# Attention values of two heads: one 128-column product, or two 64-column products on halves of the array

## The chip, the cores and the metric

The kernel runs on one core of one Trainium2 chip. The metric is the device time of one execution in microseconds (us); three runs of the kernel before gave 1727.19, 1726.89 and 1725.22 us, median 1726.89.

## The reference, cut to what matters

A two-layer encoder trunk on 512 tokens of width 1024. Each layer has three branches (a gated linear recurrence A, a spatial gating B, a windowed attention C), a gated merge, and an MLP. The change lies in branch C: eight query heads of 64 columns share two key/value heads of 64 columns; each block of 128 queries sees its own block of keys and the neighbours.

```python
def window_attention(q, k, v, sink):
    ...
    scores = jnp.einsum('bnqhgd,bnkhd->bnhgqk', qb, kb).astype(jnp.float32) * (C_HDIM ** -0.5)
    ...
    p = jnp.exp(scores - m)
    p = p / (jnp.sum(p, axis=-1, keepdims=True) + jnp.exp(sink_l - m))
    o = jnp.einsum('bnhgqk,bnkhd->bnqhgd', p.astype(v.dtype), vb)
    return o.reshape(bsz, s_len, C_QW)
```

Query head j uses the first value head and query head 4+j the second; the kernel handles the two as pair j.

## The kernel before, in words

Activations lie feature by token: 128 partitions of features, 512 tokens along the free axis. Large products are done as three float32r products of high and low parts (`mm3`, L200 to L202; the same pattern at L242 to L244 and L406 to L408). Weights come from DRAM in 512 KB pieces (L175), are rounded by ScalarE (ACT, L195) and the remainder is taken by VectorE (DVE, L196).

Branch C runs with pieces of branch A (`a_head`, L534 to L633) and the gates of branch B (`merge_b`, projections at L200 to L202 into `gz` and `yB`) in one stage per layer. For each pair j (four) and each query block n (four):

- `c_scores`: two float32r products into a bank (L912, L913) for each head, mask and maximum on DVE (L915), exponentials and sums on ACT (L919, L921), the division on DVE (L926) for one head and on ACT (L928) for the other.
- `c_out`: for each of the two heads, TensorE (PE) transposes the nb blocks of probabilities into a bank (L941), and ACT copies them into `pT`, a tile [128 keys, block, head, 128 queries] (L942). nb is 2 for the first and last query block and 3 for the two others. Then the value products (L946) and the copies into `yc` (L948).

In `c_out`, `cv[:, kb:kb + P]` holds 128 keys by 128 value columns: 64 columns of the first value head, 64 of the second. The product of L946 takes all 128 columns as weights and streams both heads' probabilities, 256 columns, so its output is 128 partitions by 256 columns. Only two quarters of it are wanted: the first head's queries on partitions 0 to 63, the second head's on 64 to 127. L948 copies these two quarters, 64 partitions by 128 columns each, into the two halves of `yc[j]`.

These products are float32; the trace shows each as two records of MATMUL with a weight load (LDWEIGHTS, listed as PEld) each. There are 4 x 4 query blocks per layer with 40 products, 80 products in both layers.

PSUM has eight banks in four groups of two; transposes of `pT` and the product `po` share group "s". `pT` has one buffer. A list scheduler sets each engine's order over the whole program, by priorities (`later`, `hp`) and its own simulated timeline; so an edit at one place can move other instructions of the stage.

Of the kernel before, what the change touches and what calls it, by code (L numbers as in the profile page):

```python
# [12 lines left out]
P = 128  # L13
# [46 lines left out]
def trunk(tc, xT, xt, ws, vec, fnb, bsb, snk, wst, rope, cmask, amask, ident, out):  # L60
    nc = tc.nc
# [30 lines left out]
    def nm(s):  # L92
        ctr[0] += 1
        return f"{s}_{ctr[0]}"

    def T(tag, name, dt=F32):
        where = part[HOME[tag]] if tag in HOME else sb
        return where.tile([P, S], dt, tag=tag, bufs=SLOTS[tag], name=nm(name))
# [17 lines left out]
    def PT(tag, name):  # L116
        return ps.tile([P, S], F32, tag="p_" + tag, bufs=BANKS[tag], name=nm(name))
# [557 lines left out]
    for l in range(DEPTH):  # L675
# [196 lines left out]
        lo64, hi64 = slice(0, 64), slice(64, 128)  # L872
# [15 lines left out]
        cv = T("ch", "cvt")  # L888
# [10 lines left out]
        yc = []  # L899
# [31 lines left out]
        def c_out(j, n, lo_, nb, Ps):  # L931
            if n == 0:
                yc.append(T("l", "yc"))


            pT = part["br"].tile([P, 3, 2, P], F32, tag="pT", bufs=1, name=nm("pT"))
            for h in range(2):
                pt = PT("s", "pT")
                for b in range(nb):
                    c = slice(b * P, (b + 1) * P)  # L940
                    nc.tensor.transpose(pt[:, c], Ps[h][:, c], id_t)  # L941
                nc.scalar.copy(pT[:, :nb, h], pt[:, :nb * P].rearrange("p (a b) -> p a b", a=nb))  # L942
            po = PT("s", "po")
            for b in range(nb):
                kb = (lo_ + b) * P
                nc.tensor.matmul(po[:, 0:2 * P], cv[:, kb:kb + P], pT[:, b].rearrange("p a b -> p (a b)"), start=b == 0, stop=b == nb - 1)  # L946
            for h, r in enumerate((lo64, hi64)):
                nc.scalar.copy(yc[j][r, n * P:(n + 1) * P], po[r, h * P:(h + 1) * P])  # L948

        def gates(tag, i, fl):  # L950

# [12 lines left out]
        def c_run(j):  # L964
            nonlocal prev
            with later(15000):
                qs = c_q(j)
                for n in range(4):
                    cur = c_scores(j, n, qs)
                    if prev is not None:  # L970
                        c_out(*prev)
                    prev = cur
# [13 lines left out]
        with later(15000):  # L986
            c_out(*prev)
# [281 lines left out]
```

## Time and profile before

| what | value |
|---|---|
| median of the runs | 1726.89 us (1725.22 to 1727.19) |
| span of the profiled execution | 1723.3 us (first to last instruction) |
| median of the runs less that span | 3.6 us |
| instructions | 21981 |
| product of L946 | 160 records, median 379 ns |
| copy of L948 | 64 records, median 260 ns |
| first and last start of L946 | 253.8 and 1293.2 us |

The profile gives no time of its own for the profiled execution beside the span, so the table sets the median of the runs beside it. In the profile each instruction has a line of the kernel, an engine, a start and a duration. PE records are pipelined: a record is longer than the distance from its start to the next one's start. A group of n like records shown as one is as long as n - 1 such distances and one record; the distance is called the pace below. A wait is put down to the instruction that ended it.

### The profile page before, as it was taken

To read this page: it belongs to the slowest core of one execution; us is meant where nothing else is said; L and a number is where in the kernel's file an instruction comes from. 1 tells how busy PE (TensorE), PEld (TensorE's weight loads), DVE (VectorE), ACT (ScalarE), POOL (GpSimd) and SP (SyncE) were. 2 spreads that over 40 slices of the span, in tenths; PEclk is the share of its full clock that TensorE was granted. 3 is DMA by queue.
4 is the path that set the end of the run, shared out by engine and by line. 5 is a ranking of instruction groups with operands and counts; after the bars stand their busy time and mean duration, and the time that the engine had idled before them with its cause. 6 is when DMAs were issued, how large, how long until landed. Compare 5 with 4: busy or idle time off the path is not lost.

```text
span 1723.3 us, 21981 instructions
## 1 busy us (share of the span) xinstructions
PE 1684.3 (98%) x8024; PEld 1405.6 (82%) x8024; DVE 1297.3 (75%) x2024; ACT 1010.9 (59%) x1705; POOL 155.1 (9%) x215
## 2 busy tenths in 40 slices
PE   7999999999999999999999999999989999999997
PEld 5888888888878888888888887888878788888886
DVE  7996987677565768687889869777875667676867
ACT  6665587676335555545666664868882355545464
POOL 1021210100310000000000112001004100000001
PEclk9999999999999999999999999999999999999999
DMA  8243222222555323222334232322216453232311
GB/s 318 75 147 115 84 86 86 86 86 74 185 213 188 98 99 110 98 98 98 135 112 137 95 115 74 104 86 98 86 43 228 169 183 105 98 110 86 122 62 49
DMA packets 58283, 200.04 MB, mean 116 GB/s; under 512 B 7904, under 2 KB 8288, under 8 KB 58176
## 3 DMA queue, kind: packets, MB, share of 16 engines
q1 hardware_dynamic: 44640, 154.72, 26.4%
q0 software_dynamic: 13248, 43.40, 6.9%
q8 instruction: 63, 1.03, 0.3%
q10 hardware_dynamic: 288, 0.52, 0.1%
q14 instruction: 44, 0.36, 0.1%
HBM read 177.64 MB, written 20.97 MB: 115 GB/s over the span
## 4 chain that ended last, share of the span: by engine, by line
PE 82%; DVE 8%; ACT 4%; issue 4%; DMA 1%; POOL 1%; SPq 0%; POOLq 0%; DVEq 0%; ACTq 0%
PE up L201 7%; PE up L200 7%; PE up L202 7%; PE dA L406 3%; PE dA L408 3%; PE dA L407 3%; PE at L534 2%; PE gz L200 2%; PE gz L201 2%; PE gz L202 2%; PE wo L243 2%; PE dC L407 2%; PE dC L406 2%; PE dC L408 2%; PE wo L244 2%
## 5 line engine op out<-in xcount | busy, mean ns | idle before, releaser
L195 ACT CAST wh<-wq 128x1024 fp32r<-128x1024 f32 x196 | 206.2, 1052 | 212.0 <-PE dA L407 49.2
L196 DVE TENSOR_TENSOR wl<-wr,wh 128x1024 fp32r<-128x1024 f32 x171 | 209.4, 1225 | 157.6 <-ACT wh L195 156.9
L195 ACT CAST wh<-wr 128x1024 fp32r<-128x1024 f32 x171 | 179.4, 1049 | 229.5 <-PE up L201 88.4
L196 DVE TENSOR_TENSOR wl<-wq,wh 128x1024 fp32r<-128x1024 f32 x196 | 239.2, 1222 | 87.7 <-ACT wh L195 86.6
L201 PE MATMUL up<-xl,wh 128*128 128x512 f32 x512 | 199.2, 390 | 0.0
L202 PE MATMUL up<-xh,wl 128*128 128x512 f32 x512 | 199.2, 390 | 0.0
L200 PE MATMUL up<-xh,wh 128*128 128x512 f32 x512 | 198.8, 389 | 0.0
L202 PEld LDWEIGHTS up<-xh,wl 128*128 128x128 f32 x512 | 96.1, 188 | 20.0
L200 PEld LDWEIGHTS up<-xh,wh 128*128 128x128 f32 x512 | 96.1, 188 | 20.0
L201 PEld LDWEIGHTS up<-xl,wh 128*128 128x128 f32 x512 | 96.1, 188 | 19.8
L406 PE MATMUL dA<-wh,sh 128*128 128x512 f32 x256 | 99.8, 390 | 0.0
L407 PE MATMUL dA<-wh,sh 128*128 128x512 f32 x256 | 99.7, 389 | 0.0
L408 PE MATMUL dA<-wl,sh 128*128 128x512 f32 x256 | 92.6, 390 | 0.0
L576 DVE TENSOR_TENSOR ex<-ex 128x512 f32<-128x512 f32 x112 | 78.4, 718 | 10.7 <-ACT kt L551 10.0
L548 ACT ACTIVATE qt<-ex 128x512 f32<-128x512 f32 x56 | 37.8, 675 | 53.6 <-DVE ex L576 41.0
L262 POOL TENSOR_TENSOR rs<-ms,mhalf_t 128x4 f32<-128x4 f32 (+2 forms) x15 | 18.9, 1257 | 516.7 <-DVE ms L260 516.7
L534 PEld LDWEIGHTS at<-qt,kt 128*128 128x128 f32 x448 | 57.5, 191 | 8.3 <-ACT kt L551 3.7
L534 PE MATMUL at<-qt,kt 128*128 128x128 f32 x448 | 59.7, 276 | 2.7 <-DVE qt L549 2.0
L406 PEld LDWEIGHTS dA<-wh,sh 128*128 128x128 f32 x256 | 48.0, 188 | 10.0
L408 PEld LDWEIGHTS dA<-wl,sh 128*128 128x128 f32 x256 | 48.1, 188 | 9.9
L407 PEld LDWEIGHTS dA<-wh,sh 128*128 128x128 f32 x256 | 48.1, 188 | 9.9
L200 PE MATMUL gz<-xh,wh 128*128 128x512 f32 x128 | 51.1, 400 | 0.0
(403 smaller groups left out, 4398.2 us busy)
## 6 DMA issues: line engine op xcount, KB each, us to landing
wr<-in_ws_dram SPq DMA_DIRECT2D x171, 512.0 KB, 3.3
wq<-in_ws_dram SPq DMA_DIRECT2D x112, 512.0 KB, 4.2
thd<-zt POOLq DMA_DIRECT2D x32, 256.0 KB, 2.6
th<-thd POOLq DMA_DIRECT2D x32, 256.0 KB, 4.2
mgd<-mg POOLq DMA_DIRECT2D x16, 256.0 KB, 2.4
mcd<-th POOLq DMA_DIRECT2D x16, 256.0 KB, 2.6
mC<-mcd POOLq DMA_DIRECT2D x16, 256.0 KB, 7.2
mB<-mgd POOLq DMA_DIRECT2D x16, 256.0 KB, 5.8
```

What stands on the lines that cost most here:

```text
L195: nc.scalar.copy(hi, raw)
L196: nc.vector.tensor_tensor(lo, raw, hi.bitcast(F32), ALU.subtract)
L200: nc.tensor.matmul(pt, whi, xhi, start=first, stop=False)
L201: nc.tensor.matmul(pt, whi, xlo, start=False, stop=False)
L202: nc.tensor.matmul(pt, wlo, xhi, start=False, stop=last)
L243: nc.tensor.matmul(pts[t], xl, hi[:, c], start=False, stop=False)
L406: nc.tensor.matmul(pt, xh[:, t], hi[:, c], start=start and k == 0, stop=False, skip_group_check=True)
L407: nc.tensor.matmul(pt, xl[:, t], hi[:, c], start=False, stop=False, skip_group_check=True)
L408: nc.tensor.matmul(pt, xh[:, t], lo[:, c], start=False, stop=k == 3, skip_group_check=True)
L534: nc.tensor.matmul(pt[:, c], kk(st), qq[:, c], start=True, stop=True)
L548: nc.scalar.activation(qt.rearrange(shp, b=nb, h=2), e_q, AF.Exp)
L576: nc.vector.tensor_tensor(o_ap, o_ap, ap_of(ex, i_, [[istep, 2]] + z), ALU.add)
```

## The change

Each product of 128 weight columns and 256 streamed columns becomes two products of 64 weight columns and 128 streamed columns. Head 0 goes to partitions 0 to 63 of the bank, head 1 to partitions 64 to 127, both in the same 128 columns. One copy of 128 partitions by 128 columns replaces the two copies.

```diff
             for b in range(nb):
                 kb = (lo_ + b) * P
-                nc.tensor.matmul(po[:, 0:2 * P], cv[:, kb:kb + P], pT[:, b].rearrange("p a b -> p (a b)"), start=b == 0, stop=b == nb - 1)
-            for h, r in enumerate((lo64, hi64)):
-                nc.scalar.copy(yc[j][r, n * P:(n + 1) * P], po[r, h * P:(h + 1) * P])
+                for h, r in enumerate((lo64, hi64)):
+                    nc.tensor.matmul(po[r, 0:P], cv[:, kb + h * 64:kb + h * 64 + 64], pT[:, b, h], start=b == 0, stop=b == nb - 1, skip_group_check=True)
+            nc.scalar.copy(yc[j][:, n * P:(n + 1) * P], po[:, 0:P])
```

In the built program every instruction of PE names the part of the array that it uses: before, all 7520 use 128 rows by 128 columns. After, 7440 do, and the 160 value products use 128 rows by 64 columns, at column 0 or at column 64.

The scheduler moves other rows too. PE, layer 0, pair 0, second query block, before: `po` is the value product, `at` an attention product of branch A, `gz` a gate projection, `pT` a transpose, `sc` scores.

```order
L912 MATMUL sc_2389<-k_399_1920,q_512_2376 128x256
L913 MATMUL sc_2389<-kl_1922,q_512_2376 128x256
L201 MATMUL gz_2968<-xl_156,wh_2964 128x512
L202 MATMUL gz_2968<-xh_155,wl_2965 128x512
L946 MATMUL po_2041<-pT_2030,cvt_1936 128x256
L534 MATMUL at_2222<-qt_2217,kt_2220 128x128 x4
L946 MATMUL po_2041<-pT_2030,cvt_1936 128x256 x2
L941 MATMUL pT_2070<-id_t,sc_2014 128x128 x3
```

The same query block after the change, where its first product stands:

```order
L941 MATMUL pT_2037<-id_t,sc_1982 128x128 x3
L947 MATMUL po_2042<-pT_2031,cvt_1936 64x128
L912 MATMUL sc_2389<-k_398_1919,q_511_2380 128x256
L534 MATMUL at_2214<-q_2196,dg_2212 128x128 x4
L913 MATMUL sc_2389<-kl_1921,q_511_2380 128x256
L201 MATMUL yB_2969<-yl_1705,wh_2915 128x512
```

And further on, where its other five stand:

```order
L534 MATMUL at_2227<-qt_2222,kt_2225 128x128 x4
L912 MATMUL sc_2394<-k_399_1920,q_512_2381 128x256
L913 MATMUL sc_2394<-kl_1922,q_512_2381 128x256
L200 MATMUL gz_2991<-xh_151,wh_2987 128x512
L947 MATMUL po_2042<-pT_2031,cvt_1936 64x128 x5
L941 MATMUL pT_2073<-id_t,sc_2015 128x128 x3
```

Before, the first product needs both heads' transposed probabilities. After, the first product of head 0 needs only head 0's, so it stands apart, and the other five follow later. Over both layers the 160 value products stand in 59 unbroken runs: 26 of one product, 2 of two, 12 of three, 6 of four, 8 of five and 5 of six.

ACT, from the copy of the first query block's result, before (`lb` are small tiles of the recurrence's bounds, `wh` a weight's high part):

```order
L948 COPY yc_1993<-po_2003 64x128 x2
L491 ACT_TABLE_LOAD
L491 ACTIVATE lb_1580<-lb_1580 128x8
L195 CAST wh_2998<-wr_2996 128x1024
L491 ACTIVATE lb_1587<-lb_1587 128x8
L844 ACT_TABLE_LOAD
L844 ACTIVATE gz_2943<-gz_2943 128x512
L554 COPY at_2193<-at_2199 128x512
L548 ACTIVATE qt_2217<-ex_2151 128x512
L551 ACTIVATE kt_2220<-ex_2151 128x512
L942 COPY pT_2030<-pT_2036 128x3x128
```

After:

```order
L948 COPY yc_1993<-po_2003 128x128
L491 ACT_TABLE_LOAD
L491 ACTIVATE lb_1580<-lb_1580 128x8
L554 COPY at_2198<-at_2204 128x512
L548 ACT_TABLE_LOAD
L548 ACTIVATE qt_2222<-ex_2156 128x512
L491 ACT_TABLE_LOAD
L491 ACTIVATE lb_1587<-lb_1587 128x8
L551 ACT_TABLE_LOAD
L551 ACTIVATE kt_2225<-ex_2156 128x512
L195 CAST wh_3021<-wr_3019 128x1024
```

The two copies of the result are one row of 128 partitions, and the functions of branch A now come between the two rows of L491, with table loads on either side. In the whole program ACT has 27 table loads before and 29 after.

## The prediction

> **What bounds the kernel now.** I read the page's busy times first, then the windows of the two stages that hold branch C, then the waits of TensorE (PE) in them, and last the records of the changed lines in order of time.
>
> ```profile
> span 1723.3 us, 21981 instructions
> PE 1684.3 (98%) x8024; PEld 1405.6 (82%) x8024; DVE 1297.3 (75%) x2024; ACT 1010.9 (59%) x1705; POOL 155.1 (9%) x215
> PE 82%; DVE 8%; ACT 4%; issue 4%; DMA 1%; POOL 1%; SPq 0%; POOLq 0%; DVEq 0%; ACTq 0%
> ```
>
> The third row is the chain that ended last. PE is busy 98% of the span and holds 82% of that chain: it is the bound, unless a stage says otherwise. The windows are layer 0's stage, most of layer 1's, and layer 1's end; the columns are length, PE, PEld, DVE, ACT and POOL.
>
> ```profile
> 200.00:460.00 260.00, 257.23 (x1390) 220.51 (x1389) 199.29 (x415) 175.42 (x388) 30.53 (x39) 1.00 0.27 92
> 1090.00:1260.00 170.00, 170.00 (x925) 146.79 (x924) 123.88 (x259) 131.36 (x277) 13.10 (x18) 1.00 0.26 87
> 1260.00:1300.00 40.00, 33.78 (x201) 28.45 (x200) 32.38 (x78) 32.46 (x84) 4.88 (x5) 1.00 0.12 37
> ```
>
> PE is idle for 2.8 us of the first window, never in the second, and 6.2 us in the third, all at the full granted clock (1.00). So whatever the change adds to PE's stream or takes from it reaches the end nearly one for one, except in the last 40 us, where ACT and DVE are each busy for 32 us and PE waits for them:
>
> ```profile
> PE po L946 <- ACT pT L942: 1.7, 1, 1.7
> PE pT L941 <- ACT yc L948: 1.5, 2, 1.1
> ```
>
> The second of these waits is for the copies that the change makes one.
>
> **The change part by part.** *The wide products go.* Their rows, and four pieces of PE's and PEld's order:
>
> ```profile
> L946 PEld LDWEIGHTS po<-pT,cvt x160: 186/190/193, 253.8 to 1293.2; 128*128 128x128 f32 x160
> L946 PE MATMUL po<-pT,cvt x160: 377/379/484, 253.9 to 1293.5; 128*128 128x256 f32 x160
> ...
> L534 PE MATMUL at<-qt,kt x448: 270/275/377, 184.2 to 1290.2; 128*128 128x128 f32 x150
> ...
> 1278.45 0.40 PE L244 MATMUL yC<-wl,yh 128*128 128x512 f32 x1
> ...
> 1278.68 1.05 PE L534 MATMUL at<-qt,kt 128*128 128x128 f32 x8
> ...
> 1279.46 1.17 PEld L946 LDWEIGHTS po<-pT,cvt 128*128 128x128 f32 x6
> 1279.57 1.46 PE L946 MATMUL po<-pT,cvt 128*128 128x256 f32 x6
> ...
> 1285.51 0.97 PEld L534 LDWEIGHTS at<-qt,kt 128*128 128x128 f32 x8 [1.09 <-ACT kt L551]
> 1285.55 1.13 PE L534 MATMUL at<-qt,kt 128*128 128x128 f32 x8 [0.88 <-DVE qt L549]
> ```
>
> The six records at 1279.57 last 1.46 us and one lasts 0.379, so the pace is (1.46 - 0.38) / 5 = 0.216 us. All 160 records hold PE for 160 x 0.216 = 34.6 us; that goes.
>
> *Narrow products come.* 160 products, 320 records by the same two for each, of 128 streamed columns. The nearest row with 128 float32 columns is the product `at`: the eight at 1278.68 give (1.05 - 0.275) / 7 = 0.111 us. If the records pass PE one behind another, 320 x 0.111 = 35.5 us come: 0.9 us more than went, since twice as many stream half as wide. If the two heads' products, which use different column halves and different partitions of the bank, pass beside each other, a slot of 0.111 us is saved wherever a product follows one of the other head. The 160 products stand in 59 unbroken runs, heads alternating, two slots to a product. Within a run the second slot of each is shared with the first of the next, so it takes one slot more than it has products: (160 + 59) x 0.111 = 24.3 us. The trace shows no two records beside each other, so the ends are 35.5 and 24.3. I take 24.3, because nothing in the operands orders the two heads: they share no weights, output or streamed columns. That is 10.3 us less than before.
>
> The Trainium skill, "TensorE: Matmul & The Clock Gate", section "Measured speedup vs the span model", reports three column tiles at 2.38 times one; two tiles at that efficiency, 1.59 times, would be an estimate of 35.5 / 1.59 = 22.3 us instead of 24.3. No run here shows it.
>
> *Changes of the array's division come.* Each run is entered from full-width work and left to it: 59 x 2 = 118 changes. What follows what costs nothing now, as long as every record is of the full array: `at` starts 0.23 us after the wider record of L244, one pace of those, and `po` starts 0.89 us after `at`, which is 8 x 0.111. So a change may cost 0. From the other side: a record lasts 0.275 us at a pace of 0.111, so 0.164 us of it lies behind its successor's start. If work in the new division may enter only when the old has left, that 0.164 us is lost at each change. If the weights can't be loaded before then either, the restart comes on top: the group at 1285.51 starts on an idle PE, and from its first weight load to the end of its last record are 1.17 us against 1.05, so 0.12 more, 0.284 in all. The ends for 118 changes are 0 and 33.5 us. I take the in-flight time alone, 118 x 0.164 = **19.4 us**: I suppose that columns still on their way through the array need the division they entered with, and the weight loads lie a pace ahead of their products (1279.46 before 1279.57), so they can be hidden. This row decides the sign: with the gain above, the break-even is 10.3 / 118 = 0.087 us a change.
>
> The Trainium skill, "TensorEngine Tiling (Array Packing)", section "Key Properties", says that a change of tiling mode drains TensorE, and gives no time for it. By that rule the term of 19.4 or 33.5 us stands; without it, it would be 0. No run here shows a change of mode.
>
> *Copies.* Two copies become one of twice the partitions; the rows are ACT's.
>
> ```profile
> L948 ACT COPY yc<-po x64: 238/260/263, 256.6 to 1294.1; 64x128 f32<-64x128 f32 x64
> L624 ACT ACTIVATE asq<-av x32: 256/277/289, 250.1 to 1304.6; 128x128 f32<-128x128 f32 x32
> L551 ACT ACT_TABLE_LOAD x2 | 2.6, 1283 | 0.0
> ```
>
> ACT reads 128 partitions by 128 columns of PSUM in 0.277 us at L624, so 64 x 0.260 = 16.6 us become 32 x 0.277 = 8.9. ACT gets 7.7 us, and its two additional table loads (27 become 29) take 2 x 1.283 = 2.6 back. Almost all of it lies under PE, which is full. Only at layer 1's end do the copies stand in the chain, as two in a row:
>
> ```profile
> 1293.88 0.26 ACT yc L948
> 1294.15 0.27 ACT yc L948
> ```
>
> There four query blocks' results or so fall in PE's waits; one copy less for each is 4 x 0.26 = 1.0 us, which I take off. If none of them decides, it is 0.
>
> *The order.* The scheduler moves some 250 of PE's rows, and DVE's and ACT's with them. Lone first products start before head 1's transposes are copied, and everything queued on PE behind one that waits for ACT would wait too; ACT then waits for PE's banks. All of PE's idle time in the three windows is 2.8 + 6.2 = 9.0 us, so a better order can give no more than that, and a worse one as much again. I take 0, since the work between is the same, and keep 4 us to either side, about half.
>
> *Sum*: 24.3 - 34.6 + 19.4 - 1.0 = 8.1 us, a span of 1731.4. The median of the runs lies 1726.9 - 1723.3 = 3.6 above the span; so 1735.0 us, 0.5% slower.
>
> **The rivals.**
>
> *The division changes for free, and the halves pass beside each other.* Then -10.3 - 1.0 = -11.3, so 1715.6 us, 0.7% faster. For it: records of different kinds and widths follow each other without a gap now, as the rows above show. Against it: in all of these the whole array is one piece. Below 0.087 us a change this side wins. Chance 0.28.
>
> *The halves don't pass beside each other*, so that the change doesn't do on PE what it says: 35.5 - 34.6 - 1.0 = -0.1 us with free changes, 1726.8 us, no change; with 0.164 us each, 1746 us. For it: in the rows above no record starts less than 0.11 us behind the one before, a 128-column record's whole pace. Against it: 0.111 is also simply the time of 128 float32 columns, half of 0.216 for 256, so streaming sets it and no fixed cost per record. Chances 0.10 and 0.14.
>
> *A full restart at each change*, with the halves side by side: 33.5 - 10.3 - 1.0 = 22.2 us, 1749 us. For it: the 0.12 us after a wait is in the row. Against it: PEld runs ahead of PE where PE is full, as at 1279.46. Chance 0.14.
>
> **How the numbers follow.** The forecast, 1735, has 0.34; with the order's 4 us to either side it runs from 1731 to 1739. A measurement of this kernel can tell about 0.2%, 3.5 us, from no change. The forecast gives slower 0.28, same 0.04, faster 0.02 (cost of a change nearer 0.08); the free change gives faster 0.26, same 0.02; no overlap with free changes gives same 0.08, slower 0.01, faster 0.01; the two others give slower 0.28. Together: faster 0.29, same 0.14, slower 0.57. The range for 8 in 10 runs from 1713 (the free change, with 3 us of better order) to 1752 (the restart, with 3 us of worse); a full restart without overlap, 1727 + 33 = 1760, is left out.
>
> **What would show it.** In the trace after, the value products are 64 weight columns by 128. Side by side: within a run of six, twelve records start about 0.055 us apart on the mean, not 0.111. Free changes: the first full-width record behind a run starts where the last narrow one's stream ends; with the in-flight cost there is a gap of 0.16, and of 0.28 with a restart, on both sides of a run. PE's total in the windows of branch C grows by 9 us or shrinks by 10. The copies show as 32 of about 0.28 us. I would be wrong through the cost of one change of division above all, since it stands 118 times in the sum and no row before shows it.

## The result and the profile after

| | before | after |
|---|---|---|
| median of the runs, us | 1727.04 (1725.22 to 1728.62) | 1739.37 (1737.30 to 1740.49) |
| ratio to before | | 1.0074, 95% interval 1.0062 to 1.0086 |
| span of the profiled execution, us | 1723.3 | 1735.5 |

The kernel became 0.7% slower; 1735.0 was forecast. First the head of the page after, then the rows of the changed lines.

```profile
span 1735.5 us, 22252 instructions
PE 1693.0 (98%) x8184; PEld 1399.3 (81%) x8184; DVE 1298.0 (75%) x2024; ACT 1003.4 (58%) x1675; POOL 157.6 (9%) x215
```

```profile
L947 PEld LDWEIGHTS po<-pT,cvt x320: 132/136/138, 253.1 to 1295.1; 128*64 128x64 f32 x160
L947 PE MATMUL po<-pT,cvt x320: 272/273/324, 253.2 to 1295.2; 128*64 128x128 f32 x160
L948 ACT COPY yc<-po x32: 242/265/282, 256.0 to 1295.5; 128x128 f32<-128x128 f32 x32
```

There are 320 narrow records of 0.273 us in place of 160 of 0.379, and 32 copies of 0.265 us in place of 64 of 0.260. Two records make one narrow product. PE is still busy for 98% of the span. Two runs of value products in PE's order of time show the price. The columns are start, duration, engine, line, operation.

```profile
252.94 0.28 PE L913 MATMUL sc<-kl,q 128*128 128x256 f32 x1
253.15 0.66 PE L947 MATMUL po<-pT,cvt 128*64 128x128 f32 x8
253.74 0.55 PE L941 MATMUL pT<-id_t,sc 128*128 128x128 f32 x3
...
258.23 0.49 PE L941 MATMUL pT<-id_t,sc 128*128 128x128 f32 x3
258.65 0.43 PE L947 MATMUL po<-pT,cvt 128*64 128x128 f32 x2
259.01 0.39 PE L912 MATMUL sc<-k,q 128*128 128x256 f32 x1
```

In the first, eight records (four products) last 0.66 us, so their pace is (0.66 - 0.273) / 7 = 0.055 us, half of the 0.111 of a 128-column float32 record on the full array: the two heads do pass beside each other. But before and behind each run PE loses time. What a run holds of PE is the distance from the end of the record ahead to the end of the group behind, less that group's own stream. The four products hold (254.29 - 3 x 0.111) - 253.22 = 0.74 us, where their records at a pace of 0.055 need 0.44. The lone product at 258.65 holds (259.40 - 0.11) - 258.72 = 0.57, where its two records need 0.22.

Medians of this measure over all runs with no wait in them: 0.57 us for a run of one or two products, 0.73 of three or four, 0.95 of five or six. Over the program's 26 + 2, 12 + 6 and 8 + 5 such runs that is **41.5 us**, against 34.3 before by the same measure (0.42, 0.86 and 1.29 us for one, two and three wide products). So the value products account for 7.2 of the 12.2 us; the rows have two decimals, so such a sum is good to about half a microsecond.

Most of the rest is in PE's waits. Those between 180 and 1400 us sum to 17.0 us before and 20.9 after. Three of the larger ones after are these (total, times, longest); the first has no like before:

```profile
PE oT L631 <- DVE ao L627: 3.3, 1, 3.3
PE po L947 <- ACT pT L942: 2.7, 4, 1.6
PE at L534 <- ACT kt L551: 1.7, 1, 1.7
```

By layers the waits rose from 5.6 to 8.7 us ahead of 1000 us, and from 11.5 to 12.2 behind it. In layer 0 the third of these and 1.8 us of the second are new. The third goes with ACT's new order, which sets two table loads, 2.6 us, between the function that makes `qt` and the one that makes `kt`. In columns as above:

```profile
261.09 1.28 ACT L491 ACT_TABLE_LOAD   x1
262.38 0.21 ACT L491 ACTIVATE lb<-lb 128x8 f32<-128x8 f32 x1
262.61 1.28 ACT L551 ACT_TABLE_LOAD   x1
263.90 0.68 ACT L551 ACTIVATE kt<-ex 128x512 f32<-128x512 f32 x1
```

PE's products of `kt` start right behind, at 264.64, after PE has stood idle for 1.71 us; the kernel before has neither loads nor a wait there. In layer 1 the first of the three, 3.3 us, mostly took the place of waits that went. PE's order there, at the layer's end:

```profile
1317.65 0.39 PE L619 MATMUL av<-st,qd 128*128 128x128 f32 x2
1321.32 0.66 PE L631 MATMUL oT<-id_t,ao 128*128 128x128 f32 x4 [3.28 <-DVE ao L627]
...
1323.34 0.63 PE L243 MATMUL yA<-wh,yl 128*128 128x512 f32 x1
1323.77 0.63 PE L244 MATMUL yA<-wl,yh 128*128 128x512 f32 x1
```

After the last head's last `av` product its norm runs through ACT, POOL and DVE, and PE has nothing else: a bare tail, as it is called below. In the kernel before, products of `yC` stand at this place:

```profile
1303.43 0.39 PE L619 MATMUL av<-st,qd 128*128 128x128 f32 x2
1303.57 0.48 PE L242 MATMUL yC<-wh,yh 128*128 128x512 f32 x1
1303.89 0.40 PE L243 MATMUL yC<-wh,yl 128*128 128x512 f32 x1
```

In the program's order 34 products of 512 columns (all but one of them `yC`), 7.8 us of PE work at 0.23 us each, stand between this `av` and `oT` before, and none after. Behind the wait the products start 0.43 us apart (1323.34 to 1323.77) instead of 0.23. Windows of 2 us show why; the number behind the bracket is the granted clock, which fell to half:

```profile
1322.00:1324.00 2.00, 1.45 (x4) 0.66 0.11 14
1324.00:1326.00 2.00, 2.00 (x6) 0.50 0.86 297
1326.00:1328.00 2.00, 2.00 (x10) 0.99 0.93 279
```

### The profile page after: what moved, and what is told of

The parts are those of the page before. It is cut to its first block, busy times and chain, and to the rows that moved or that the text cites. A ratio compares the mean times of both kernels' runs of the same rounds, so it can differ in the third digit from the quotient of the medians.

```text
span 1735.5 us, 22252 instructions
## 1 busy us (share of the span) xinstructions
PE 1693.0 (98%) x8184; PEld 1399.3 (81%) x8184; DVE 1298.0 (75%) x2024; ACT 1003.4 (58%) x1675; POOL 157.6 (9%) x215
## 4 chain that ended last, share of the span: by engine, by line
PE 80%; DVE 7%; issue 4%; ACT 4%; DMA 3%; POOL 1%; SPq 0%; POOLq 0%; ACTq 0%; DVEq 0%
PE up L200 7%; PE up L201 7%; PE up L202 7%; PE dA L406 3%; PE dA L407 3%; PE dA L408 3%; PE at L534 2%; PE wo L243 2%; PE wo L244 2%; PE dC L407 2%; PE dC L406 2%; PE dC L408 2%; PE wo L242 2%; PE po L947 2%; PE gz L201 1%
## 5 line engine op out<-in xcount | busy, mean ns | idle before, releaser
L202 PEld LDWEIGHTS up<-xh,wl 128*128 128x128 f32 x512 | 96.2, 188 | 20.1
L200 PEld LDWEIGHTS up<-xh,wh 128*128 128x128 f32 x512 | 96.2, 188 | 19.8
L243 PE MATMUL wo<-wh,mgl 128*128 128x512 f32 x128 | 51.2, 401 | 0.1
```

Source lines behind the costliest of these rows:

```text
L200: nc.tensor.matmul(pt, whi, xhi, start=first, stop=False)
L202: nc.tensor.matmul(pt, wlo, xhi, start=False, stop=last)
L243: nc.tensor.matmul(pts[t], xl, hi[:, c], start=False, stop=False)
```

## The experiments

Every kernel was run beside the kernel before; ratios are to it. The table puts each profiled span beside three measures of it, as differences from the kernel before: value products (the medians by length of run times the runs in the program, as above), PE's waits between 180 and 1400 us, and what the granted clock lost between 100 and 1400 us (one minus the clock, summed over windows of 2 us; an upper bound, since PE was idle in part of them). The spans are of one execution each: their differences lie up to 4.4 us above those of the medians (e9) and up to 1.5 below (e2). The three measures don't add up to the span either; what they leave lies between -4 and +3 us.

| kernel | median, us | span | value products | waits | clock, up to |
|---|---|---|---|---|---|
| before | 1727.04 | 1723.3 | 34.3 | 17.0 | 1.7 |
| after | 1739.37 | +12.2 | +7.2 | +3.9 | +3.4 |
| e1 head 1 first | 1731.60 | +4.6 | -4.9 | +7.0 | +3.4 |
| e2 full array, narrow | 1729.97 | +1.4 | +1.5 | +2.5 | 0.0 |
| e3 one half | 1746.06 | +20.8 | +20.5 | -0.7 | +5.1 |
| e5 after, gates last | 1748.70 | +24.7 | +5.2 | +12.1 | +10.3 |
| e6 before, gates last | 1739.04 | +13.9 | 0.0 | +9.1 | +5.1 |
| e7 pairs | 1734.84 | +9.9 | -7.8 | +7.6 | +13.6 |
| e8 head 1 first, A early | 1732.03 | +7.5 | -5.7 | +9.3 | +3.4 |
| e9 zero-padded | 1735.46 | +12.8 | +1.5 | +8.2 | +5.1 |
| e10 pairs, heads first | 1715.19 | -10.3 | -10.8 | -2.4 | +6.8 |
| e11 before, heads first | 1744.74 | +19.0 | 0.0 | +10.9 | +5.1 |
| e12 after, heads first | 1736.21 | +11.1 | +6.7 | +2.8 | +1.7 |

### The disputed cost by itself (e4)

```diff
+        H(*[0, 1] * 20)      # halves in turn
+        H(*[0] * 40)         # one half
+        for _ in range(20):  # full and half in turn
+            F()
+            H(0)
```

> Leaves out the whole trunk: it only runs rows of products on two loaded tiles and writes zeros. Rows of 128-column float32 products: full array alone, halves in turn, one half alone, full and half in turn, pairs, four after two, and the same behind 512-column float32r products. Theory (a change of the array's division costs about 0.18 us, as the changed kernel's runs show, and the two halves pass beside each other): 40 full products take 40 x 0.222 = 8.9 us, 40 in turn on two halves about half, 4.5 us, 40 on one half 8.9 us; 20 times full and half in turn 8.9 + 40 x 0.18 = 16 us. Rival (changes are free, the loss lies in waits of the new order): that last row takes 8.9 us. Second rival (the halves don't overlap): the halves in turn take 8.9 us.

The groups, in order: full array, 512-column products, halves in turn, one half, full and half in turn, two and two, two full ones and four on halves, two on halves behind two 512-column products, and two full ones behind two 512-column products, which is a row without any change of division. A product is two records, but for the 512-column ones.

```profile
23.00 6.86 PE L83 MATMUL full<-x,w 128*128 128x128 f32 x60
29.61 2.98 PE L79 MATMUL warm<-xr,wr 128*128 128x512 f32 x12
32.52 4.59 PE L87 MATMUL half<-x,w 128*64 128x128 f32 x80
...
39.98 8.95 PE L87 MATMUL half<-x,w 128*64 128x128 f32 x80
...
52.02 0.43 PE L87 MATMUL half<-x,w 128*64 128x128 f32 x2
52.38 0.49 PE L83 MATMUL full<-x,w 128*128 128x128 f32 x2
52.80 0.43 PE L87 MATMUL half<-x,w 128*64 128x128 f32 x2
...
70.63 0.44 PE L87 MATMUL half<-x,w 128*64 128x128 f32 x4
...
71.64 0.44 PE L87 MATMUL half<-x,w 128*64 128x128 f32 x4
...
93.62 0.66 PE L87 MATMUL half<-x,w 128*64 128x128 f32 x8
...
94.85 0.66 PE L87 MATMUL half<-x,w 128*64 128x128 f32 x8
...
120.98 0.44 PE L87 MATMUL half<-x,w 128*64 128x128 f32 x4
...
140.61 0.44 PE L87 MATMUL half<-x,w 128*64 128x128 f32 x4
...
144.30 0.60 PE L83 MATMUL full<-x,w 128*128 128x128 f32 x4
...
161.53 0.61 PE L83 MATMUL full<-x,w 128*128 128x128 f32 x4
```

The paces are (6.86 - 0.275) / 59 = 0.112 us on the full array, (4.59 - 0.273) / 79 = 0.055 on the halves in turn, and (8.95 - 0.273) / 79 = 0.110 on one half. Full and half in turn repeat every 0.78 us (52.02 to 52.80), with streams of 2 x 0.111 + 2 x 0.110 = 0.44: 0.34 for two changes, **0.17 us each** on the mean. Two and two repeat every 1.01 us, (1.01 - 0.44 - 4 x 0.055) / 2 = 0.17; two and four every 1.23, (1.23 - 0.44 - 8 x 0.055) / 2 = 0.17; two behind two 512-column products, whose pace is (2.98 - 0.39) / 11 = 0.235 us here, every (140.61 - 120.98) / 19 = 1.033, (1.033 - 0.47 - 0.22) / 2 = 0.17. The cost is the same behind both kinds of products. The last row, with as many alternations of 512 and 128 columns but all on the full array, repeats every (161.53 - 144.30) / 19 = 0.907 us, and 0.907 - 0.47 - 0.44 = 0.00: an alternation of the kind of product alone costs nothing. Both rivals fall.

PEld shows where it goes. In the same row of products, weight loads:

```profile
52.02 0.19 PEld L87 LDWEIGHTS half<-x,w 128*64 128x64 f32 x2
52.38 0.30 PEld L83 LDWEIGHTS full<-x,w 128*128 128x128 f32 x2 [0.17 <-issue]
```

The load of the new division starts with its products (52.02 and 52.38, as the MATMULs above), not a pace ahead of them, and PEld waits 0.17 us for nothing that the profile names. Part of the 0.34 us lies ahead of the first record in the new division, and part behind it: two records at the usual pace would take 0.275 + 0.11 = 0.38, but the pair on a half takes 0.43 and the pair on the full array 0.49.

### Narrow on the full array (e2), and on one half (e3)

```diff
-                    nc.tensor.matmul(po[r, 0:P], cv[:, kb + h * 64:kb + h * 64 + 64], pT[:, b, h], ...)
+                    nc.tensor.matmul(po[:, h * P:(h + 1) * P], cv[:, kb:kb + P], pT[:, b, h], ...)
```

> The 160 narrow products and their split order, but on the full array: 128 weight columns, 128 streamed columns for each head, two copies as before. No change of division and no overlap. Theory: 35.5 us of stream instead of 34.6, 0.9 us more than before, plus what the order costs, 0 to 5 us: 1728 to 1733 us. Rival (the order is what costs): 1736 to 1740 us, as the changed kernel.

```diff
-                    nc.tensor.matmul(po[r, 0:P], cv[:, kb + h * 64:kb + h * 64 + 64], pT[:, b, h], ...)
+                    nc.tensor.matmul(po[lo64, h * P:(h + 1) * P], cv[:, kb + h * 64:kb + h * 64 + 64], pT[:, b, h], ...)
```

> As the full-array narrow kernel, in the same order on every engine, but with 64 weight columns, both heads on partitions 0 to 63 of the bank (two copies, the second to the other half of yc). 124 changes of division, no overlap. Theory: 124 x 0.18 = 22 us over the full-array narrow kernel: about 1751 us. Rival (changes are free): the same time as the full-array narrow kernel, within 2 us.

Measured: 1729.97 us, ratio 1.0020 (1.0011 to 1.0028), and 1746.06, ratio 1.0112 (1.0097 to 1.0128). Every engine has the same instructions in the same order in the two, so their difference, 19.4 us between the spans and 16.1 between the medians, comes from the division: over 124 changes 0.13 to 0.16 us each, a little under the 0.18 that was expected. By the measure of the value products alone it is 19.0 us, 0.15 each. The same four products, on the full array and on one half:

```profile
253.41 1.05 PE L947 MATMUL po<-pT,cvt 128*128 128x128 f32 x8
254.30 0.27 PE L941 MATMUL pT<-id_t,sc 128*128 128x128 f32 x1
```

```profile
254.69 1.09 PE L947 MATMUL po<-pT,cvt 128*64 128x128 f32 x8
255.71 0.33 PE L941 MATMUL pT<-id_t,sc 128*128 128x128 f32 x1
```

From the eight records' start to the next start are 0.89 us in the first, 8 paces of 0.111, and 1.02 in the second. Halving the columns and splitting the order cost little by themselves; the changes of division are shown to be what costs. That the overlap then gives back some is seen between e3 and the changed kernel: their value products differ by 54.8 - 41.5 = 13.3 us, at 124 and 118 changes.

### Fewer changes: head 1 first (e1)

```diff
-                for h, r in enumerate((lo64, hi64)):
+                for h, r in ((1, hi64), (0, lo64)):
```

> In every block head 1's product goes first, so a query block's products become ready together. The program has 38 unbroken runs and 76 changes of division instead of 59 and 118. Theory: with the times of the changed kernel's own runs (0.57 us for one or two products, 0.74 for three or four, 0.95 for five or six) the value products hold TensorE for 29.8 us instead of 41.5, so about 12 us less than the changed kernel: 1727 us, and some more off if the waits of the order shrink too. Rival (changes are free and the loss is the lone early product's waits): the 5 us of waits and order go, 1734 us. Rival (half-width records are slow by themselves): no change, 1739 us.

Measured: 1731.60 us, ratio 1.0028 (1.0017 to 1.0039), where 1727 was expected. The value products fell to 29.4 us, as expected, below the kernel before. But the waits grew by 7.0 us, with half clock behind two of them, and the kernel stayed slower than before, although no tail is bare in it. The term was right and the order took more than it gave.

### The bare tail (e5, e6)

```diff
             for h in range(4):
-                gate_a()
-
             ys = y_split(yc, "yh")
 ...
                     nc.gpsimd.dma_start(mcd[:, fl * 4 + t], th[t])
+            for h in range(4):
+                gate_a()
         ys = []
```

> The changed kernel with branch A's four gate projections written behind the yC products instead of ahead of them. By the program's order 7.8 us of TensorE work then stand between the last head's last av product and its transposes oT in layer 1 (as in the kernel before), where the changed kernel has none. 110 changes of division instead of 118. Theory (7.0 us of the loss are TensorE's time for the products and their changes, the rest is this uncovered tail with the half clock behind it): 5 to 6 us off for the tail and 1.4 for the 8 changes: about 1732 us. Rival (the changes of division are the whole loss): 1.4 us off, 1738 us.

> Control: the kernel before with the same move of the gate projections. Its tail in layer 1 had cover already. Theory (only the lack of cover makes the move worth something): within 2 us of the kernel before, 1725 to 1729 us. Rival (the move helps by itself): 1720 us.

Both missed: 1748.70 us, ratio 1.0123 (1.0108 to 1.0138), and 1739.04, ratio 1.0070 (1.0058 to 1.0083). The move covered the tail and opened other waits; in the kernel before it alone costs 12 us. As a repair it fails. As a comparison it goes some way: with the tail covered in both, the changed kernel is 24.7 - 13.9 = 10.8 us of span behind the other (9.7 between the medians), of which 5.2 are the value products and 3.0 waits: nearly as far as with the tail bare.

### Two query blocks together (e7), and other orders (e8, e10, e11, e12)

```diff
+            pend.append((lo_, nb, pT))
+            if len(pend) < 2:
+                return
             po = PT("s", "po")
+            for i in range(2 - 1, -1, -1):
+                lo2, nb2, pT2 = pend[i]
+                ...
+                    for h, r in ((1, hi64), (0, lo64)):
+                        nc.tensor.matmul(po[r, i * P:(i + 1) * P], ..., pT2[:, b, h], ...)
+            pend.clear()
+            nc.scalar.copy(yc[j][:, (n + 1 - 2) * P:(n + 1) * P], po[:, 0:2 * P])
```

> Two query blocks' value products stand together, head 1 first, with one copy of 256 columns for both; the transposed probabilities of one block of each two lie in another buffer. 27 runs, 54 changes of division. Theory: by the changed kernel's run times continued at 0.2 us for two more products, the value products hold TensorE for 26 us, 8 less than before and 15 less than in the changed kernel; but the program's order leaves the last head of each layer without cover (0 and 1.4 us of work), which costs 5 to 10 us: 1724 to 1729 us. Rival (changes are free): the changed kernel's time but for the order, 1736 to 1740 us.

Measured: 1734.84 us, ratio 1.0044 (1.0032 to 1.0057). The value products fell to 26.5 us as expected; the waits and the half clock of bare tails cost more than the 5 to 10 us that were set for them.

```diff
-        head(2)
-        fill(3,4)
-        head(3)
+        head(2)
+        head(3)
+        fill(3,4)
```

> Head 1's product first, as in the run of that name, and branch A's last head written ahead of two gate products: 37 runs, 74 changes of division, at least 7.7 us of cover behind every head of branch A. Theory: the value products hold TensorE for 28.7 us by the run times, 5.9 less than before, and no tail is bare: about 1721 us. Rival (the rest of the loss is not in bare tails but in the half-width products' own waits): 1731 us, as the run with head 1 first alone.

Measured (e8, on e1): 1732.03 us, ratio 1.0032 (1.0021 to 1.0043). The value products came to 28.6 us, as expected, and no tail was bare; yet the time is that of its rival, 1731, and the waits grew by 9.3 us. The theory that a bare tail is the order's whole cost falls. Of the 9.3, 5.1 are, as the rival had it, waits of the value products themselves for the copies into `pT` (6.8 us, against 1.7 before); the rest lies in other places.

```diff
-        c_run(0)
-        head(1)
-        c_run(1)
-        c_run(2)
-        c_run(3)
-        fill(0,1,2)
-        with later(15000):
-            c_out(*prev)
-        head(2)
-        fill(3,4)
+        head(1)
+        c_run(0)
+        c_run(1)
+        fill(0,1,2)
+        head(2)
+        c_run(2)
+        c_run(3)
+        with later(15000):
+            c_out(*prev)
+        fill(3,4)
         head(3)
```

This order on the pairs (e10), on the kernel before (e11) and on the changed kernel (e12):

> The pairs again, with branch A's heads written ahead in the program, so that 4 to 11 us of work stand behind every head's last product; 19 runs, 38 changes of division. Theory: by the run times the value products hold TensorE for 23 us instead of 34.3, so 11 us less than the kernel before; if the waits come out as before's, 1716 us, and with 5 us more of them and of half clock, as in the other reordered kernels, 1721 us. Rival (the halves cost waits of their own whatever the order): 1732 us or more, as the other runs on halves.

> Control: the kernel before with the same order of branch A's heads and branch C's pairs. No change of division. Theory (the scheduler's new order by itself is worth nothing or costs): 1727 to 1735 us, so that the pairs' gain over this one is about 11 us. Rival (the new order is what helps the pairs): as fast as the pairs.

> The changed kernel with the program order of branch A's heads and branch C's pairs that the two runs before this one had: 57 runs, 114 changes of division. Theory (the value products cost by their runs and changes, whatever the order): they hold TensorE for 40.8 us by the run times, 6.5 more than in the kernel before; with the waits of the kernel before in the same order, 1751 us, and 36 us more than the pairs, of which 17 are the value products' own. Rival (the halves, not the grouping, make the new order good): about 1720 us, near the pairs.

Measured: 1715.19 us, ratio 0.9937 (0.9923 to 0.9950); 1744.74, ratio 1.0104 (1.0090 to 1.0118); 1736.21, ratio 1.0059 (1.0045 to 1.0073). The pairs in this order beat both kernels. Two of their runs:

```profile
1240.01 1.31 PE L952 MATMUL po<-pT,cvt 128*64 128x128 f32 x18
...
1251.06 1.31 PE L952 MATMUL po<-pT,cvt 128*64 128x128 f32 x20
1252.30 0.44 PE L912 MATMUL sc<-k,q 128*128 128x384 f32 x1
```

These are nine and ten products; either run lasts 1.31 us, with two changes of division. By the medians a run of ten holds PE for 1.39 us, against 2.15 for the five wide products that they replace (5 x 0.43). All value products take 23.5 us, 10.8 less than before, and PE waits 2.4 us less. The control e11, with the same program order and wide products, is 17.7 us slower than before, 10 more than was expected at most, so the order by itself is no gain. Against e12, on halves and in this order but not in pairs, the pairs gain 21.0 us, 17.5 of them in the value products. e12 came 15 us below its expectation: its value products cost 6.7 us more than before, as expected, but PE's waits didn't carry over from e11 (19.8 us against 27.9). What the order costs has to be measured for each kernel.

### One copy without halves (e9)

```diff
+        cz = [T("ch", "cz"), T("ch", "cz")]
 ...
+                    nc.tensor.matmul(po[:, 0:P], cz[h][:, kb:kb + P], pT[:, b, h], start=b + h == 0, stop=b + h == nb)
 ...
-            with later(15000):
+            with later(18000):
                 qs = c_q(j)
```

This edit is of the changed kernel. In each tile `cz[h]` the other head's 64 columns are zero.

> One copy per result without any change of division: two tiles of value columns, each with the other head's 64 columns zero, so both heads' products use the full array and add up in the same 128 columns; branch C written 18000 later instead of 15000 in the scheduler's priorities. Theory: 0.9 us more of stream than before, the copies' 8 us on ScalarE are worth about 1 us, and the order gives or takes a few: 1724 to 1732 us; no row of a value product behind or ahead of a 0.17 us gap. Rival (the single copy with its narrow products was the loss): 1735 us or more.

Measured: 1735.46 us, ratio 1.0052 (1.0040 to 1.0065), above the expected range and at the time of the rival. But the value products are not the loss: runs of one to six hold PE for 0.23, 0.45, 0.67, 0.89, 1.12 and 1.34 us, within 0.01 us of e2. Waits are up by 8.2 us, half of the rise in the largest one (PE's wait for `mC`, 4.1 us). The single copy's 8 us of ACT brought nothing that shows; since the edit also moved branch C in the scheduler's priorities, its worth by itself stays open.

## Why the prediction was right, and where it was off

**Direction and size.** 8.1 us slower were forecast; the spans differ by 12.2 and the medians by 12.3. The 1739.37 us lie just beyond the 1731 to 1739 that the order's 4 us gave, and well within the range for 8 in 10. The errors partly cancel: the overlap was taken 2.9 us too high, and the order some 5 too low.

**Cost of a change of division**, 118 x 0.164 = 19.4 us: right. The step took the in-flight time of a record; e4 measured 0.17 us a change, 118 x 0.17 = 20.1. The rival with a restart on top, 0.284 us each, falls; so does the free change. The mechanism behind the number is shown only in part. The step supposed that the weight loads are hidden, and that the whole 0.164 us lie ahead of the first record of the new division. In e4 the loads start with their products, and of the 0.34 us for two changes 0.05 + 0.10 lie behind that first record. So the size of the in-flight time came out with some luck: no run varies it enough to show that it is what is waited for.

**Overlap**, 24.3 us of stream: right in kind, a little too high. Of the 41.5 us, less 20.1 for the changes, 21.4 are stream. The step let a run take one slot more than it has products; in the trace a run of two holds PE no longer than a run of one (0.57 us), so two products pass wholly beside each other. The estimate by three tiles' efficiency, 22.3, was nearer than the 24.3 that was taken, but by luck: two tiles in turn are 2.0 times as fast as one in e4 (0.055 against 0.110), not 1.59, and what they lose is at the products that stand alone.

The rule on which the prediction weighed this, that a change of tiling mode drains TensorE while tiles of one mode run beside each other (the Trainium skill, "TensorEngine Tiling (Array Packing)", section "Key Properties"), agrees with e4 in both halves: 0.17 us a change, and 0.055 us for two tiles in turn against 0.110 for one.

**Copies**, 1.0 us off: not seen. PE's waits for `yc` (1.5 us before) are gone, but its waits for the copies into `pT` rose from 1.7 to 3.9 (2.7 at `po`, 1.2 at the transposes). The two additional table loads, which were put under PE, did reach it: 1.7 us at 264.64.

**Order**, taken as 0 with 4 us to either side: the step that was mis-sized. It measured 3.9 us of waits and up to 3.4 of half clock behind them. The prediction bounded the waits by PE's idle time before, which bounds what a better order can give but not what a worse one can take, and counted no clock. Its windows also end at 1300 us, ahead of the bare tail and both new steps at half clock. It did name the way in which 1.6 us came: at 440.64 five products waited for a copy into `pT` behind a lone first product. The other kernels show how wide this term really is: waits from -2.4 to +12.1 us, in stages whose other work was the same but for its order.

**What stays open.** Why the scheduler left the tail bare is not known from these runs; e5 took the tail away and lost more elsewhere. That the missing 1.1 us of the span (12.2 less 7.2 and 3.9) are the half clock is argued from the rows at 1322 us, not shown by a kernel without it; the clock may have cost up to 3.4, and what would then offset the rest is not known.

## What to carry to other kernels

Products on halves of the array do run two at a time, but entering and leaving a run of them costs 0.17 us each here, on the mean, so a run must be long: against the wide products that they replace two lose (0.57 us for 0.43), four gain a little (0.73 for 0.86) and ten gain a third (1.39 for 2.15). Count the runs in the program's order rather than the products in the code, since a product that becomes ready early will stand alone. And where a scheduler sets the order, hold an edit's own term apart from the waits that the new order opens; a control with the same order tells them apart only as far as its waits are the same.

## What was not expected of the hardware

The granted clock fell to half after short waits: behind the 3.28 us wait, and again behind two smaller ones. PE's order there:

```profile
1348.08 0.96 PE L242 MATMUL wo<-wh,mgh 128*128 128x512 f32 x3 [1.15 <-ACT mgh L250]
1349.42 0.50 PE L242 MATMUL wo<-wh,mgh 128*128 128x512 f32 x1 [0.37 <-DVE mB L1026]
```

Between 100 and 1400 us the traces of the thirteen trunk kernels have 37 stretches at half clock. Within a trace they start whole multiples of 3.413 us apart (1322.64 and 1349.95: eight) and last one to three such steps. Cut into these steps, the kernel after looks like this; the columns are length, PE's busy time, granted clock, DMA:

```profile
1319.23:1322.64 3.41, 0.88 (x5) 1.00 0.00 0
1346.54:1349.95 3.41, 1.85 (x8) 1.00 0.82 311
1349.95:1353.36 3.41, 3.34 (x8) 0.50 0.82 264
```

And the kernel before, with waits of the same kind at that place:

```profile
1332.95:1336.36 3.41, 2.74 (x19) 1.00 0.99 375
1336.36:1339.77 3.41, 2.69 (x14) 1.00 1.03 376
```

So in these traces the clock goes by PE's idle time in a step more than by the length of one wait. Ahead of the two half-clock steps PE was idle for 2.53 and 1.56 us; the kernel before was idle for 1.4 us too, but 0.67 in one step and 0.72 in the next, and its clock stayed at 1.00. In this stretch of all thirteen traces, every step at full clock with more than 1.9 us of idle time was followed by half clock and none with less than 1.28; between these it came out either way. Where a wait falls on the steps thus decides in part what it costs. The Trainium skill, "TensorE: Matmul & The Clock Gate", section "HAM oscillation — how this bites in real kernels", gives idle gaps of 3.4 us as the limit; the first wait here, 3.28 us, lies near it, the second case, 1.5 us in two pieces, well below, and the clock fell behind both.
